# Sparse experts: in three of eight groups the expert with the fewest tokens changes places with the last one, and the last one is put into the conditional second round

## The chip, the cores and the metric

The kernel runs on one core of a Trainium2 chip. The metric is device time in microseconds for one execution; lower is better. Several runs of a kernel are given by their median.

## The reference

The reference is two transformer blocks on 256 tokens of width 1024, all in fp32. The first block is dense. The second has a mixer and then a mixture of experts, which is what the change is about:

```python
MOE_GROUPS, EXPERTS_PER_GROUP, TOP_K, D_FF_EXPERT = 8, 8, 2, 512
group_logits = t @ w_router_group                      # 256 x 8
g_sel   = argmax(group_logits)                         # one group for a token
in_group = (t @ w_router_expert).reshape(n, 8, 8)[rows, g_sel]
top_logit, top_local = lax.top_k(in_group, 2)          # two experts of that group
gate = softmax(top_logit) * softmax(group_logits)[g_sel]
...
hid = silu(xb @ w_gate[e]) * (xb @ w_up[e])            # 1024 -> 512
y  += gate * (hid @ w_down[e])                         # 512 -> 1024
```

There are 64 experts. The three matrices of one have 3 x 1024 x 512 fp32 values, 6.29 MB. The 256 tokens give 512 pairs of token and expert, so an expert has 8 tokens on average, and some may have none.

## The kernel before

Everything up to the mixture of experts is the same in both kernels. The experts run in `moe` (L1339), from about 657 us to about 1630 us of the profile.

Groups are processed as **visits**. `plan` (L1120) counts the tokens of each group and sorts them: group 0 is always at place 0, the others follow by size at places 1 to 7. `which` (an int32 copy of `at_`) holds the group at each place. The first visit is group 0 with experts 0 to 2, whose names are known without any counting; then come places 1, 2, 3, 7, 4, 5, 6 with eight experts each, and last group 0 again with experts 3 to 7. That makes 64 expert steps, numbered i = 0 to 63. `in_order` (L1499) gives the index of an expert for a load, from a register that SP reads from `which`.

A group at places 0 to 6 is "small": 64 token slots. Each small group's tokens are gathered by a matmul with a one-hot matrix (`prepare`, L1221; `slot2`, `keys`), split into a high and a low fp32r part and held as the 128 stationary columns `xghi` (64 slots, high and low). Place 7 has 128 slots and three passes in place of two. After the last expert of a visit `summed` (L1317) scatters the result into `xres`.

One expert step is 12 chunks: four of `w_gate`, four of `w_up`, four of `w_down` of the expert before. A chunk (128 x 1024) is split by ACT (`whi`) and DVE (`wlo`) in `split` (L104, L107), except that the fourth chunk of `w_down` is used as it is (L1389). The chunks are fetched three ahead (`AHEAD`). There are six buffers of `whi` and `wlo`. From chunk s = 8 on, the order of PE, ACT and DVE is the order of the program text; before it a scheduler orders them, and what stands under `soon()` has priority.

The weights are loaded by SP in six DMAs of 1 MB for an expert, into a ring of 11 slots (L1492 to L1496). SP issues in program order, and a load waits until its slot has been read. A load carries a condition from the third expert on (`wanted`, L1267): SP reads the number of the expert's tokens from `manyx` into a register, and where it is 0 the DMA is issued but moves nothing. The rest of the expert's step is carried out all the same, on whatever the slot holds, with gate weights of zero.

`weights` (L1093) computes the gate weights `wsel` (token x expert in its group), `count` (L1194) the tokens of each expert, `beyond` (L1156) whether a group has more tokens than slots, in small DVE instructions that are mixed into the steps from s = 121 on. `flag` is 1 when some group has. Then a **second round** (L1516 to L1518) runs two more groups, 16 experts with 128 slots; else it is jumped over.

Of the kernel before, what the change touches and what calls it, by code (L numbers as in the profile page):

```python
# [9 lines left out]
F32 = mybir.dt.float32  # L10
# [22 lines left out]
def mega(ctx, tc, a, out, dbg=None):  # L33
# [1059 lines left out]
    def weights():  # L1093
# [23 lines left out]
        nc.vector.tensor_tensor(wsel, o1, o2, op=OP.add)  # L1117
        dump("wsel", wsel)

    def plan():  # L1120
        ps = mm.tile([P, 512], F32, tag="mm", name="pct")
        for t in range(NT):
            nc.tensor.matmul(ps[:, :8], ones, G[:, t, :], start=t == 0, stop=t == 1)

        c64 = lambda n: mp.tile([P, 8, 8], F32, name=n)
        col = lambda x: x[:, :, None].to_broadcast([P, 8, 8])
        lin = lambda x: x[:, None, :].to_broadcast([P, 8, 8])
        size = mp.tile([P, 8], F32, name="size")
        nc.vector.scalar_tensor_tensor(size, ps[:, :8], 16.0, rdx, op0=OP.mult, op1=OP.add)
        nc.vector.memset(size[:, 0:1], -1.0)  # L1130
        gidx = mp.tile([P, 8], F32, name="gidx")
        nc.vector.tensor_scalar(gidx, rdx, -1.0, 8.0, op0=OP.mult, op1=OP.add)
        perm = c64("perm")
        nc.vector.tensor_tensor(perm, lin(size), col(size), op=OP.is_lt)
        place = mp.tile([P, 8], F32, name="place")
        nc.vector.tensor_reduce(place, perm, AX.X, OP.add)

        nc.vector.tensor_scalar(base, place, NG - 1.0, float(P - GS), op0=OP.is_equal, op1=OP.mult)
        nc.vector.tensor_scalar(base, base, float(GS), None, op0=OP.add)
        nc.vector.tensor_tensor(over, ps[:, :8], base, op=OP.subtract)  # L1140
        nc.vector.tensor_tensor(perm, col(gidx), lin(place), op=OP.is_equal)
        work = c64("work")
        nc.vector.tensor_tensor(work, perm, lin(gidx), op=OP.mult)
        at_ = mp.tile([P, 8], F32, name="at_")
        nc.vector.tensor_reduce(at_, work, AX.X, OP.add)
        nc.vector.tensor_copy(which, at_)
        for t in range(NT):
            nc.vector.tensor_tensor(work, perm, lin(G[:, t, :]), op=OP.mult)
            nc.vector.tensor_reduce(keys[:, t, :], work, AX.X, OP.add)
        nc.vector.tensor_copy(keys_, keys)  # L1150
        nc.vector.tensor_scalar(keys, keys, -4096.0, 4096.0, op0=OP.mult, op1=OP.add)
        nc.vector.tensor_tensor(keys, keys, b8(rank), op=OP.add)
# [3 lines left out]
    def beyond():  # L1156

        b1 = lambda n, w=1: mp.tile([P, w], F32, name=n)
        r, at, ovi, off, mem = b1("bey_r", 8), b1("bey_at", 8), b1("ovi", 3), b1("bey_off"), r8("bey_mem")
        nc.vector.tensor_scalar(r, over, 0.0, None, op0=OP.is_gt)  # L1160
        nc.vector.tensor_tensor(r, r, rdx, op=OP.mult)
        for x in range(2):
            m, key = ovi[:, 1 + x:2 + x], keyx[x]
            nc.vector.tensor_reduce(m, r, AX.X, OP.max)
            if x:
                nc.vector.tensor_scalar(off, over[:, 0:1], float(P), None, op0=OP.is_gt)
                nc.vector.tensor_scalar(at[:, 0:1], off, 8.0, None, op0=OP.mult)
                nc.vector.tensor_tensor(m, m, at[:, 0:1], op=OP.max)
                nc.vector.scalar_tensor_tensor(base[:, 0:1], off, float(P), base[:, 0:1], op0=OP.mult, op1=OP.add)
            else:  # L1170
                nc.vector.tensor_scalar(ovi[:, 0:1], m, 0.0, None, op0=OP.is_gt)
            yield
            nc.vector.tensor_tensor(at, rdx, m.to_broadcast([P, 8]), op=OP.is_equal)
            for t in range(NT):
                nc.vector.tensor_tensor(mem[:, t, :], G[:, t, :], at, op=OP.mult)
            nc.vector.tensor_reduce(key, mem, AX.X, OP.add)
            nc.vector.tensor_scalar(key, key, -4096.0, 4096.0, op0=OP.mult, op1=OP.add)
            nc.vector.tensor_tensor(key, key, rank, op=OP.add)
            yield
            nc.vector.tensor_tensor(mem[:, 0, :], at, base, op=OP.mult)  # L1180
            nc.vector.tensor_reduce(off, mem[:, 0, :], AX.X, OP.add)
            nc.vector.tensor_tensor(key, key, off.to_broadcast([P, NT]), op=OP.subtract)
            if x == 0:
                nc.vector.tensor_tensor(at, at, r, op=OP.mult)
                nc.vector.tensor_tensor(r, r, at, op=OP.subtract)
            yield
        nc.vector.tensor_scalar(ovi[:, 1:3], ovi[:, 1:3], -1.0, 8.0, op0=OP.mult, op1=OP.add)
        nc.vector.tensor_scalar(ovi[:, 1:3], ovi[:, 1:3], NG - 1.0, None, op0=OP.min)
        nc.vector.tensor_copy(ovx, ovi)
        for _ in range(6):  # L1190
            yield
        beyonds["flag"] = nc.values_load(ovx[0:1, 0:1], min_val=0, max_val=1, skip_runtime_bounds_check_because="it is 0 or 1")

    def count():  # L1194

        for t in range(NT):
            nc.vector.tensor_tensor(sel[:, t], keys_[:, t, :, None].to_broadcast([P, 8, 8]),
                                    osel[:, t, None, :].to_broadcast([P, 8, 8]), op=OP.mult)
        ps = mm.tile([P, 512], F32, tag="mm", name="pct")
        for t in range(NT):  # L1200
            nc.tensor.matmul(ps[:, :64], ones, sel[:, t].rearrange("p g e -> p (g e)"), start=t == 0, stop=t == 1)
        nc.vector.tensor_copy(manyx, ps[:, :64])

    ev = lambda w: w.rearrange("e (p k) n -> p e k n", p=P)
    wg, wu, wd = ev(a["w_gate_2"]), ev(a["w_up_2"]), ev(a["w_down_2"])
# [12 lines left out]
    def two(x):  # L1218
        return x.rearrange("p k (a b) -> p k a b", a=2)

    def prepare(keys, b, small, xgs, gws, v):  # L1221

        oh = mq.tile([P, NT, P], F32, name="oh", bufs=1)
        for t in range(NT):
# [111 lines left out]

    AHEAD = 3

    def moe(keys, expert, visits, small=lambda g: False, skip=False, begin=(), on_the_way=iter(())):  # L1339

        todo = [(v, g, e, es) for v, (g, es) in enumerate(visits) for e in es]
        n = len(todo)
        plain = lambda i: skip and small(todo[i][1]) and i < n - 2
# [70 lines left out]
        def follow(s):  # L1417

            i, kind, c = order[s]
            v, g, e, es = todo[i]  # L1420
            last = s + 1 == len(order) or order[s + 1][:2] != (i, kind)
            if kind in "gu":
                if last:
                    steps.append([1, copied(i, kind)])
                if kind == "u" and last and e == es[max(0, len(es) - 4)] and v + 1 < len(visits):
                    g2 = visits[v + 1][0]
                    steps.append([1, prepare(keys(g2), (v + 1) % 2, small(g2), xgs, gws, v + 1)])
                if i == 0 and kind == "u" and last:
                    finish(steps)
                    steps.append([1, turned(hids, 0, gus.pop(0), gws[v][0], small(g), plain(0))])  # L1430
                return
            if i + 1 < n and (last if i + 2 < n else c == 1):
                g1 = todo[i + 1][1]
                hl = None
                if i + 2 == n:
                    finish(steps)
                    hl = [x[:, (todo[i + 1][0] + 1) % 2, :4] for x in xgb]
                x = turned(hids, i + 1, gus.pop(i + 1), None, small(g1), plain(i + 1), hl)
                if i + 2 == n:
                    finish([[0, x]])  # L1440
                else:
                    steps.append([next(x), x])
            if last and e == es[-1] and i < n - 1:
                steps.append([1, summed(pds.pop(v), gws[v][1])])
# [5 lines left out]
            gens.clear()  # L1450

        with soon():
            prep = prepare(keys(visits[0][0]), 0, small(visits[0][0]), xgs, gws, 0)
            while 0 not in xgs:
                next(prep)
            for f in begin[:2]:
# [40 lines left out]
    bases = {}  # L1497

    def in_order(g, e):  # L1499
        if g == 0:  # L1500
            return e
        if g not in bases:
            bases[g] = value(which[0:1, g:g + 1], NG - 1)
        return bass.ds(bases[g] * NE + e, 1)
# [1 line left out]

    every = list(range(NE))
    moe(lambda g: [(keys[:, t, g:g + 1] if g else key0[:, t:t + 1]) for t in range(NT)], in_order,
        [(0, every[:3])] + [(g, every[3 * (g == 0):]) for g in (1, 2, 3, 7, 4, 5, 6, 0)],
        small=lambda g: g < NG - 1, skip=True, begin=(plan, weights, count), on_the_way=beyond())  # L1510


    flag = beyonds["flag"]
    again = [nc.values_load(ovx[0:1, x:x + 1], engines=(mybir.EngineType.SP,), min_val=0, max_val=NG - 1,
                            skip_runtime_bounds_check_because="a group's index") for x in (1, 2)]
    with tc.If(flag > 0):  # L1516
        moe(lambda x: [keyx[x][:, t:t + 1] for t in range(NT)], lambda x, e: bass.ds(again[x] * NE + e, 1),
            [(0, every), (1, every)])  # L1518
    dump("h2", xres)
    g_nf = row(a["norm_final_2"], D, "g_nf")  # L1520
    ms = [mean_sq(ssf[:, t, :]) for t in range(NT)]
# [54 lines left out]
```

## Time and profile before

| | |
|---|---|
| three runs | 1646.37 us median (1645.75 to 1648.77) |
| the profiled execution | 1646.35 us, of which the trace spans 1644.6 us |
| mean granted TensorE clock | 0.989 of full speed |
| PE, DVE, ACT busy | 98%, 82%, 70% of the span |

PE is TensorE's matmuls, PEld its weight loads, DVE is VectorE, ACT ScalarE, POOL GpSimd, SP SyncE. Busy time of PE is modelled from pipelined matmuls. The trace says for each instruction when it began, how long it took, and what ended the idle time before it.

### The profile page before, as it was taken

To read this page: it belongs to the slowest core of one execution; us is meant where nothing else is said; L and a number is where in the kernel's file an instruction comes from. 1 tells how busy PE (TensorE), PEld (TensorE's weight loads), DVE (VectorE), ACT (ScalarE), POOL (GpSimd) and SP (SyncE) were. 2 spreads that over 40 slices of the span, in tenths; PEclk is the share of its full clock that TensorE was granted. 3 is DMA by queue.
4 is the path that set the end of the run, shared out by engine and by line. 5 is a ranking of instruction groups with operands and counts; after the bars stand their busy time and mean duration, and the time that the engine had idled before them with its cause. 6 is when DMAs were issued, how large, how long until landed. Compare 5 with 4: busy or idle time off the path is not lost. (4 is left out here: it accounts for less than half of the span.)

```text
span 1644.6 us, 24374 instructions
## 1 busy us (share of the span) xinstructions
PE 1606.0 (98%) x8474; PEld 1302.4 (79%) x8474; DVE 1353.3 (82%) x1643; ACT 1148.5 (70%) x1544; POOL 44.7 (3%) x69
## 2 busy tenths in 40 slices
PE   8999999999999998999999999999999999999996
PEld 7898788998798877777767777778877777777774
DVE  6666675555868886799999999998999899999997
ACT  5355554444556643788878888877788888888886
POOL 1000010000100130000000000000000000000000
PEclk9999999999999998999999999999999999999999
DMA  9953455555663337797997999999999999999991
GB/s 323 273 175 130 142 171 201 180 189 170 173 182 122 116 132 298 271 421 325 385 392 315 380 421 421 421 412 363 347 380 420 409 421 420 421 420 420 421 375 48
DMA packets 124884, 493.55 MB, mean 300 GB/s; under 512 B 9149, under 2 KB 53537, under 8 KB 78160
## 3 DMA queue, kind: packets, MB, share of 16 engines
q1 hardware_dynamic: 120160, 484.47, 76.9%
q0 software_dynamic: 1952, 6.05, 1.3%
q10 hardware_dynamic: 2640, 1.38, 0.3%
q8 instruction: 69, 1.13, 0.3%
q14 instruction: 63, 0.52, 0.1%
HBM read 509.30 MB, written 1.44 MB: 311 GB/s over the span
## 5 line engine op out<-in xcount | busy, mean ns | idle before, releaser
L107 DVE TENSOR_TENSOR wlo<-ring,whi 128x1024 fp32r<-128x1024 f32 x714 | 839.9, 1219 | 63.4 <-ACT whi L107 59.8
L107 ACT CAST whi<-ring 128x1024 fp32r<-128x1024 f32 x714 | 712.3, 1048 | 74.0 <-PE pgu L1279 20.9
L1279 PE MATMUL pgu<-whi,xghi 128*128 128x512 f32 x896 | 356.6, 398 | 1.4 <-DVE xghi L1216 1.4
L1280 PE MATMUL pgu<-wlo,xghi 128*128 128x512 f32 x896 | 352.8, 394 | 1.1 <-DVE wlo L107 1.1
L107 DVE TENSOR_TENSOR wlo<-raw,whi 128x1024 fp32r<-128x1024 f32 x173 | 211.8, 1232 | 135.6 <-ACT whi L107 134.3
L107 ACT CAST whi<-raw 128x1024 fp32r<-128x1024 f32 x173 | 180.3, 1048 | 188.9 <-PE pb L115 81.0
L1280 PEld LDWEIGHTS pgu<-wlo,xghi 128*128 128x128 f32 x896 | 169.4, 189 | 37.4 <-DVE wlo L107 3.4
L1279 PEld LDWEIGHTS pgu<-whi,xghi 128*128 128x128 f32 x896 | 169.4, 189 | 35.3 <-DVE xghi L1216 1.6
L114 PE MATMUL pb<-hThi,whi 128*128 128x256 f32 x480 | 137.5, 286 | 0.2 <-ACT hThi L129 0.2
L1279 PE MATMUL pd<-whi,hidThi 128*128 128x512 f32 x332 | 136.5, 411 | 0.9 <-DVE hidThi L1299 0.8
L115 PE MATMUL pb<-hTlo,whi 128*128 128x256 f32 x480 | 135.8, 283 | 0.5 <-DVE hTlo L130 0.5
L116 PE MATMUL pb<-hThi,wlo 128*128 128x256 f32 x480 | 135.7, 283 | 0.0
L1280 PE MATMUL pd<-wlo,hidThi 128*128 128x512 f32 x332 | 130.9, 394 | 0.0
L1289 PEld LDWEIGHTS pht<-pairs,gu 128*128 128x128 f32 x896 | 108.6, 191 | 4.9
L1289 PE MATMUL pht<-pairs,gu 128*128 128x64 f32 x896 | 106.0, 271 | 0.0
L1389 PE MATMUL pd<-ring,hs 128*64 128x512 f32 x216 | 104.2, 605 | 0.0
L1279 PEld LDWEIGHTS pd<-whi,hidThi 128*128 128x128 f32 x332 | 62.2, 187 | 52.8 <-ACT whi L107 36.1
L115 PEld LDWEIGHTS pb<-hTlo,whi 128*128 128x128 f32 x480 | 91.9, 191 | 1.4 <-DVE hTlo L130 0.7
L114 PEld LDWEIGHTS pb<-hThi,whi 128*128 128x128 f32 x480 | 91.9, 191 | 1.2 <-ACT hThi L129 0.5
L116 PEld LDWEIGHTS pb<-hThi,wlo 128*128 128x128 f32 x480 | 91.8, 191 | 0.0
L114 PE MATMUL pa<-whi,hThi 128*128 128x512 f32 x216 | 87.0, 406 | 3.3 <-ACT whi L107 1.7
L116 PE MATMUL pa<-whi,hTlo 128*128 128x512 f32 x216 | 85.6, 399 | 1.2 <-DVE hTlo L130 1.2
(432 smaller groups left out, 2260.1 us busy)
## 6 DMA issues: line engine op xcount, KB each, us to landing
ring<-in_w_gate_dram SPq DMA_DIRECT2D x128, 1024.0 KB, 9.9
ring<-in_w_up_dram SPq DMA_DIRECT2D x128, 1024.0 KB, 10.6
ring<-in_w_down_dram SPq DMA_DIRECT2D x126, 1024.0 KB, 9.2
raw<-in_w_in_dram SPq DMA_DIRECT2D x38, 1024.0 KB, 5.4
raw<-in_w_ff_dram SPq DMA_DIRECT2D x32, 1024.0 KB, 5.0
raw<-in_w_out_dram SPq DMA_DIRECT2D x12, 1024.0 KB, 5.0
raw<-in_w_in_dram SPq DMA_DIRECT2D x9, 512.0 KB, 4.8
raw<-in_w_ple_gate_dram SPq DMA_DIRECT2D x4, 1024.0 KB, 5.0
```

The costliest lines, as they stand in the source:

```text
L107: both = [nc.scalar.copy(hi, raw), nc.vector.tensor_tensor(lo, raw, hi.bitcast(F32), op=OP.subtract)]
L114: nc.tensor.matmul(ps, l[0][lsel], r[0][rsel], start=first, stop=False)
L115: nc.tensor.matmul(ps, l[0][lsel], r[1][rsel], start=False, stop=False)
L116: nc.tensor.matmul(ps, l[1][lsel], r[0][rsel], start=False, stop=last)
L1279: nc.tensor.matmul(ps, x[0][:, k, :], w[0][wsel], start=first, stop=False)
L1280: nc.tensor.matmul(ps, x[0][:, k, :], w[1][wsel], start=False, stop=last)
L1289: nc.tensor.matmul(ps[:, j, q, :], x[:, ts(q)], pairs, start=True, stop=True)
L1389: nc.tensor.matmul(pds[v][m][:GS, :], h[:, 3, :], wt[:, 0, cols(m)], start=False, stop=False)
```

## The change

`count` still counts the tokens of each expert, but in a float tile `many`. For the places 0, 1 and 2 (`NS = 3`) it finds the expert with the fewest tokens, the one with the higher index first where several have as few (in group 0 experts 0 to 2 are left out, since their loads have begun by then). `trade` exchanges that expert's column with column 7, in the counts, in the names of the experts and, for the tokens of these groups, in the gate weights. The names go to `namesx`, the exchanged gate weights to `wsel2`, and the largest of the three counts that now stand in column 7 to `left`.

The first round then runs 7 experts in place of 8 in the visits of places 1 and 2, and 4 in place of 5 in the last visit of group 0: 61 steps in place of 64. The expert of column 7 of these three groups moves behind the condition of the second round, as three `moe` calls of one expert each. `flag` is 1 when a group has too many tokens or `left` is above 0.

```diff
@@ plan: at_ is made outside, the 64-wide tiles get a tag each
+    at_ = mp.tile([P, 8], F32, name="at_")
@@ beyond
-                nc.vector.tensor_scalar(ovi[:, 0:1], m, 0.0, None, op0=OP.is_gt)
+                nc.vector.tensor_tensor(ovi[:, 0:1], m, left, op=OP.max)
+                nc.vector.tensor_scalar(ovi[:, 0:1], ovi[:, 0:1], 0.0, None, op0=OP.is_gt)
@@
+    def trade(x, at, n):
+        d, both = mp.tile([P, n, 8], F32, name="trd"), mp.tile([P, n], F32, name="trs")
+        nc.vector.tensor_tensor(d, x[:, :, 7:8].to_broadcast([P, n, 8]), x, op=OP.subtract)
+        nc.vector.tensor_tensor(d, d, at, op=OP.mult)
+        nc.vector.tensor_reduce(both, d, AX.X, OP.add)
+        nc.vector.tensor_tensor(x, x, d, op=OP.add)
+        nc.vector.tensor_tensor(x[:, :, 7], x[:, :, 7], both, op=OP.subtract)
@@ count
-        nc.vector.tensor_copy(manyx, ps[:, :64])
+        many = mp.tile([P, 8, 8], F32, tag="work", name="many")
+        nc.vector.tensor_copy(many, ps[:, :64].rearrange("p (g e) -> p g e", g=8))
+        few2 = mp.tile([P, 2, NS, 8], F32, tag="perm", name="few")
+        few, few3 = few2[:, 0], few2[:, 1]
+        by3 = lambda x: x[:, None, :].to_broadcast([P, NS, 8])
+        nc.vector.scalar_tensor_tensor(few, many[:, :NS], 16.0, by3(rdx), op0=OP.mult, op1=OP.add)
+        nc.vector.memset(few[:, 0, :3], 1e6)
+        fewest = mp.tile([P, NS], F32, name="fewest")
+        nc.vector.tensor_reduce(fewest, few, AX.X, OP.min)
+        nc.vector.tensor_tensor(few, few, fewest[:, :, None].to_broadcast([P, NS, 8]), op=OP.is_equal)
+        names = mp.tile([P, NS, 8], F32, name="names")
+        nc.vector.tensor_scalar(names, by3(rdx), -1.0, 8.0, op0=OP.mult, op1=OP.add)
+        trade(many[:, :NS], few, NS)
+        trade(names, few, NS)
+        nc.vector.scalar_tensor_tensor(names, at_[:, :NS, None].to_broadcast([P, NS, 8]), 8.0, names, op0=OP.mult, op1=OP.add)
+        nc.vector.tensor_copy(manyx, many.rearrange("p g e -> p (g e)"))
+        nc.vector.tensor_copy(namesx, names)
+        nc.vector.tensor_reduce(left, many[:, :NS, NE - 1], AX.X, OP.max)
+        mine = mp.tile([P, NT, 8], F32, tag="ing", name="mine")
+        for t in range(NT):
+            nc.vector.tensor_tensor(few3, few, keys_[:, t, :NS, None].to_broadcast([P, NS, 8]), op=OP.mult)
+            nc.vector.tensor_reduce(mine[:, t, :], few3.rearrange("p g e -> p e g"), AX.X, OP.add)
+        nc.vector.tensor_copy(wsel2, wsel)
+        trade(wsel2, mine, NT)
@@ prepare takes wsel as an argument: the first visit's is wsel, the later ones' wsel2
@@ in_order
-        if g == 0:
-            return e
+        if g < NS:
+            return bass.ds(value(namesx[0:1, g, e:e + 1], NG * NE - 1), 1) if g or e > 2 else e
@@ the visits
-        [(0, every[:3])] + [(g, every[3 * (g == 0):]) for g in (1, 2, 3, 7, 4, 5, 6, 0)],
+        [(0, every[:3])] + [(g, every[3 * (g == 0):NE - (g < NS)]) for g in (1, 2, 3, 7, 4, 5, 6, 0)],
@@ behind the first round
+    lasts = [nc.values_load(namesx[0:1, x, NE - 1:NE], engines=(mybir.EngineType.SP,), min_val=0, max_val=NG * NE - 1,
+                            skip_runtime_bounds_check_because="an expert's index") for x in range(NS)]
     with tc.If(flag > 0):
+        for x in range(NS):
+            moe(lambda g: [(keys[:, t, g:g + 1] if g else key0[:, t:t + 1]) for t in range(NT)],
+                lambda g, e: bass.ds(lasts[g], 1), [(x, [NE - 1])], small=lambda g: True)
         moe(lambda x: [keyx[x][:, t:t + 1] for t in range(NT)], lambda x, e: bass.ds(again[x] * NE + e, 1),
-            [(0, every), (1, every)])
+            [(0, every), (1, every)], wsel=wsel)
```

## Rows read from the trace of the kernel before

**Rows 1.** The page's busy time by engine, share of the span, count.
```profile
PE 1606.0 (98%) x8474; PEld 1302.4 (79%) x8474; DVE 1353.3 (82%) x1643; ACT 1148.5 (70%) x1544; POOL 44.7 (3%) x69
```

**Rows 2.** Windows: length, busy PE, PEld, DVE, ACT, POOL, clock, DMA share, GB/s.
```profile
1537.32:1551.25 13.93, 13.93 (x65) 10.43 (x65) 13.26 (x14) 12.32 (x16) 0.00 (x0) 1.00 1.01 418
775.07:896.69 121.62, 119.56 (x559) 88.58 (x559) 114.79 (x147) 100.38 (x124) 0.00 (x0) 1.00 0.91 363
896.69:1014.31 117.62, 117.62 (x559) 89.33 (x559) 111.00 (x116) 101.17 (x125) 0.00 (x0) 1.00 0.99 401
1273.68:1391.22 117.54, 117.54 (x559) 89.32 (x559) 110.71 (x115) 100.59 (x124) 0.00 (x0) 1.00 1.01 416
1391.22:1508.79 117.57, 117.57 (x559) 89.32 (x559) 110.71 (x115) 100.58 (x124) 0.00 (x0) 1.00 1.01 421
```

**Rows 3.** Timeline of SP's queue late in the visit of place 6: start, length, what.
```profile
1537.32 1.16 SPq L99 DMA_DIRECT2D ring<-in_w_down_dram  x2
...
1551.25 1.05 SPq L99 DMA_DIRECT2D ring<-in_w_down_dram  x2
```

**Rows 4.** Tile ring, gate loads in 598:759, 759:763, 881:885, 1566:1571; ns min/median/max.
```profile
L99 SPq DMA_DIRECT2D ring<-in_w_gate_dram x18: 327/333/508, 598.6 to 748.3; - x18
...
L99 SPq DMA_DIRECT2D ring<-in_w_gate_dram x2: 79/86/92, 759.6 to 761.9; - x2
...
L99 SPq DMA_DIRECT2D ring<-in_w_gate_dram x2: 84/84/84, 881.8 to 883.7; - x2
...
L99 SPq DMA_DIRECT2D ring<-in_w_gate_dram x2: 84/84/84, 1567.2 to 1569.5; - x2
```

**Rows 5.** Tile ring, landing times, windows 740:760, 1180:1200, 1240:1260, 1480:1500, 1560:1566.
```profile
DMA to landing us min/median/max: 10.8/11.0/11.1
...
DMA to landing us min/median/max: 4.9/5.0/5.1
...
DMA to landing us min/median/max: 9.2/9.4/9.6
...
DMA to landing us min/median/max: 15.9/16.1/16.3
...
DMA to landing us min/median/max: 16.5/17.4/18.4
```

**Rows 6.** Tile ring over the whole span: casts and the loads of w_down.
```profile
L107 ACT CAST whi<-ring x714: 1032/1048/1071, 620.7 to 1625.8; 128x1024 fp32r<-128x1024 f32 x179
...
L99 SPq DMA_DIRECT2D ring<-in_w_down_dram x130: 84/333/1020, 612.2 to 1603.9; - x130
```

**Rows 7.** Timeline around `count`: start, length, what.
```profile
659.35 0.22 DVE L1202 CAST manyx<-pct 128x64 int32<-128x64 f32 x1 [0.39 <-PE pct L1201]
...
661.39 1.23 DVE L107 TENSOR_TENSOR wlo<-ring,whi 128x1024 fp32r<-128x1024 f32 x1 [1.81 <-ACT whi L107]
...
667.13 0.47 PE L1280 MATMUL pgu<-wlo,xghi 128*128 128x512 f32 x1
...
668.50 0.47 PE L1280 MATMUL pgu<-wlo,xghi 128*128 128x512 f32 x1
```

**Rows 8.** Timeline of DVE: two stretches of small instructions, in `plan` and `beyond`.
```profile
653.71 0.22 DVE L1148 TENSOR_TENSOR work<-perm,G 128x64 f32<-128x64 f32 x1
...
654.73 0.17 DVE L1150 COPY keys__6020<-keys 128x16 f32<-128x16 f32 x1
...
814.43 0.16 DVE L1173 TENSOR_TENSOR bey_at<-rdx,ovi 128x8 f32<-128x8 f32 x1
...
816.16 1.23 DVE L107 TENSOR_TENSOR wlo<-ring,whi 128x1024 fp32r<-128x1024 f32 x1
```

**Rows 9.** SP: its register loads, and its queue in the visit of place 7.
```profile
L1259 SPq TENSOR_LOAD <-manyx x61: 263/269/293, 668.3 to 1581.6; - x61
...
1105.33 3.07 SPq L99 DMA_DIRECT2D ring<-in_w_down_dram  x2
...
1122.29 0.33 SPq L99 DMA_DIRECT2D ring<-in_w_down_dram  x1
```

More of the change, by code (lines that the diff above doesn't have):

```diff
@@ L1123, in plan @@
             nc.tensor.matmul(ps[:, :8], ones, G[:, t, :], start=t == 0, stop=t == 1)
-        c64 = lambda n: mp.tile([P, 8, 8], F32, name=n)
+        c64 = lambda n: mp.tile([P, 8, 8], F32, tag=n, name=n)
         col = lambda x: x[:, :, None].to_broadcast([P, 8, 8])
@@ L1143, in plan @@
         nc.vector.tensor_tensor(work, perm, lin(gidx), op=OP.mult)
-        at_ = mp.tile([P, 8], F32, name="at_")
         nc.vector.tensor_reduce(at_, work, AX.X, OP.add)
@@ L1192, in beyond @@
         beyonds["flag"] = nc.values_load(ovx[0:1, 0:1], min_val=0, max_val=1, skip_runtime_bounds_check_because="it is 0 or 1")
+    NS = 3
+    namesx = mp.tile([P, NS, 8], I32, name="namesx")
+    left = mp.tile([P, 1], F32, name="left")
+    wsel2 = r8("wsel2")
+    def trade(x, at, n):
[5 more added lines that the diff above has]
+        nc.vector.tensor_tensor(x[:, :, 7], x[:, :, 7], both, op=OP.subtract)
     def count():
@@ L1219, in two, with prepare @@
         return x.rearrange("p k (a b) -> p k a b", a=2)
-    def prepare(keys, b, small, xgs, gws, v):
+    def prepare(keys, b, small, xgs, gws, v, wsel):
         oh = mq.tile([P, NT, P], F32, name="oh", bufs=1)
@@ L1337, in mega, with moe @@
     AHEAD = 3
-    def moe(keys, expert, visits, small=lambda g: False, skip=False, begin=(), on_the_way=iter(())):
+    weights_ = wsel
+    def moe(keys, expert, visits, small=lambda g: False, skip=False, begin=(), on_the_way=iter(()), wsel=wsel2):
+        first = weights_ if skip else wsel
         todo = [(v, g, e, es) for v, (g, es) in enumerate(visits) for e in es]
@@ L1426, in follow @@
                     g2 = visits[v + 1][0]
-                    steps.append([1, prepare(keys(g2), (v + 1) % 2, small(g2), xgs, gws, v + 1)])
+                    steps.append([1, prepare(keys(g2), (v + 1) % 2, small(g2), xgs, gws, v + 1, wsel)])
                 if i == 0 and kind == "u" and last:
@@ L1452, in moe @@
         with soon():
-            prep = prepare(keys(visits[0][0]), 0, small(visits[0][0]), xgs, gws, 0)
+            prep = prepare(keys(visits[0][0]), 0, small(visits[0][0]), xgs, gws, 0, first)
             while 0 not in xgs:
```

## The prediction

> **What bounds the kernel now.** The first view is the busy time by engine: PE 98%, DVE 82% [rows 1]. That is an average over a long dense part too, so the second view is the windows of the expert stage alone. One expert step in the middle of a visit takes 13.93 us, for which PE is busy without a gap (65 matmuls), DVE for 13.26 us, ACT for 12.32 us, and the DMA engines all of it, at 418 GB/s [rows 2]. Three resources are full or nearly so, and this view does not say which of them sets the pace.
>
> The third view, the loads, does. An expert is 6.29 MB; at 421 GB/s that is 6.29 / 0.421 = 14.94 us of DMA, yet steps follow each other every 13.93 us, read off the same load of successive experts in SP's queue [rows 3]. So compute runs ahead of the DMA inside a visit, and the DMA catches up at the visits' ends: eight experts take 117.54 or 117.57 us, that is 8 x 13.93 = 111.4 and 6.1 more for gathering and scattering, 14.69 us for an expert [rows 2]. The DMA still loses 0.25 us an expert. The time from issue to landing shows it: 9.2 to 9.6 us early in the visit of place 4, 15.9 to 16.1 two visits later, 17.4 at its worst [rows 5]. Does anyone wait for it? A slot comes round after 11 loads, 11/6 x 13.93 = 25.5 us; it is held while it is read, two casts of 1.05 and the subtract behind them, some 3.5 us. A load has therefore about 22 us (an estimate from these rows). The last loads agree: issued up to 1603.9, the last chunk cast at 1625.8, 21.9 us later [rows 6]. 17.4 is below 22: compute sets the pace, and PE within it.
>
> Who is empty? A load whose condition fails takes 79 to 92 ns to issue instead of 333. The first such pair of gate loads follows 18 full ones, so it is expert step 9; the second is at 881.8, 122 us or eight steps on, step 17; the third at 1567.2, step 62 [rows 4]. These are the seventh experts of places 1 and 2 and of group 0. The reference's router on its own inputs says the same: groups of 12, 22, 40, 36, 46, 17, 6 and 77 tokens, and the only three experts of all 64 with none are number 6 of groups 0, 6 (place 1) and 5 (place 2). An empty expert gets no bytes but all its compute: the stretch 896.69 to 1014.31, in which step 17 is computed, has the same 559 matmuls and takes 117.62 us, as against 117.54 where all eight have tokens [rows 2].
>
> **The change, part by part.** *Removed:* three expert steps. In each of the three groups the fewest is 0 tokens, it changes places with expert 7, and `left` is 0. What goes is 3 x 13.93 = 41.79 us of compute [rows 2, 3] and 18 loads that moved nothing. The gathering and scattering at the visits' ends stay, as the number of visits does. `todo` still ends in two steps with fully split `w_down`, so the tail is built as before.
>
> *What the DMA does then.* The same 61 experts are loaded, in less time. Until now an empty expert gave the DMA a pause: landing was at 11.0 us at 740 to 760, before step 9 [rows 5]. Without pauses a visit of seven takes 7 x 13.93 + 6.1 = 103.6 us and needs 7 x 14.94 = 104.6 of DMA, so landing grows by 1.0 in each of the first two and by 2.0 in the one of place 3: from 11 to about 15. In the visit of place 7 a step takes 1122.29 - 1105.33 = 16.96 us [rows 9], and the DMA empties its queue; landing is back at 5 by 1180 [rows 5]. From there nothing changes until step 62, whose pause is gone. There the queue is 18.4 us behind, and six more loads at 2.49 against 2.32 us add 1: 19.4, under 22. Counted as bytes: loads issued at 1565.9 go out 27.9 us earlier, at 1538, and land by 1556.4; the 8 MB that follow need 8 x 2.49 = 19.9, so all has landed by 1576.3, and the last cast is due at 1625.8 - 41.8 = 1584.0. I cost it at 0; the cover is 2.6 to 7.7 us.
>
> The Trainium skill, page "DMA: Bandwidth & Descriptors", section "Where 436 GB/s comes from", speaks against the change: for loads from HBM it lets the HBM side bind at about 358 GB/s. By that an expert would need 17.6 us, DMA would be the bound, and dropping experts without bytes would give nothing. The trace disagrees, with 421 GB/s held over whole visits [rows 2]; what the rule would do here is the second rival below.
>
> *Added in `count`:* 30 DVE instructions for 1, nearly all in a chain. Not in the trace; by the nearest rows, four 64-wide ones take (654.73 - 653.71)/4 = 0.255 us each, eleven of 8 elements (816.16 - 814.43)/11 = 0.157 [rows 8]. These have 24 to 64, so 30 take 4.7 to 7.7 us; I take 6.0. They begin when the counts come, at 659.35, and end at 665.4; the subtract that began at 661.39 is held back by 4.0 us [rows 7]. It makes the seventh chunk (the first six fill the buffers), which PE multiplies at 667.13, and it would now end at 666.6; the eighth, needed at 668.50, at 667.8. So it is nearly hidden: 0, and 1.1 at the long end. Without that cover all of it counts: at the price of `beyond`, where 32 more DVE instructions (147 against 115) cost 121.62 - 117.57 = 4.05 us, 0.127 each [rows 2], 29 would be 3.7. I take 0.6. SP's reads of `manyx` and `namesx` come long after, since the loads of step 3 wait for slots.
>
> *Moved: `beyond`.* It is tied to s = 121, the middle of step 10. That was the last step of place 1; now it is the first of place 2, and the scatter of the ended visit follows at once. DVE has 0.67 us to spare in a step, and a visit's end gives it 110.71 - 8 x 13.26 = 4.6 us of work more, as against 6.1 for PE [rows 2]. At best the two overlap (6.1 - 4.6 = 1.5 gained), at worst all 4.6 falls on the path. In an undisturbed visit PE's 6.1 covers DVE's 4.6, so I stay near that end: 1.0, and 0.1 for the one instruction more.
>
> *Added on SP:* 18 register reads from `namesx` and 3 of `lasts`, less 2 of `which`, at 0.27 us [rows 9], 5.1 us over 950, in a queue that waits for slots. Behind such a read stands one gate load, late by at most 0.27 us, a tenth of the narrowest margin above: 0. *In the second round:* code that is jumped over, by the same one branch: 0.
>
> **The sum** is made against the profiled execution, 1646.35 us, 0.02 below the median of the three runs: 1646.35 - 41.79 + 0.6 + 1.1 = 1606.3.
>
> **The rivals.**
> *The second round runs* (slower). It decides as soon as one of the three traded experts has a single token. Then `flag` is 1, and not only three experts run but all of the second round: 16 steps at 16.96 and three visits of one expert at 13.93 + 6.1, 271 + 60 = 331 us, about 1937. Against it stand the three skipped loads, one in each of the three groups [rows 4].
> *The loads set the pace, and nothing is gained.* All 61 experts with tokens are loaded as before; were DMA the bound, the time stayed at 1646. For it: DMA is full in nearly every window at 421 GB/s. Against it: the stretches with and without an empty expert take the same time, and landing stays under 22 us.
> *The loads become the bound at the end.* If the lead is 17 and not 22, the last experts wait up to 19.4 - 17 = 2.4 us, and the visit of place 3 not at all: about 1609.
> *The small DVE work is all exposed:* 3.7 for `count` and 4.6 for `beyond` on a visit's end in place of 1.6: 1646.35 - 41.79 + 8.4 = 1613.0; half of it is likelier than the whole, about 1609.5.
> *`beyond` falls in better than before:* 1.5 gained, `count` hidden: 1603.1.
>
> **How the numbers follow.** The sum as worked out, 1604 to 1608: 0.70. DVE exposed, 1608 to 1613: 0.12. Loads binding at the end: 0.06. Better placed, 1602.8 to 1604: 0.06. Loads set the pace: 0.03. Second round: 0.03. The forecast is 1606.3. The range takes in the best case and DVE's exposure up to 1612: 1602.8 to 1612.0. A measurement of this kernel tells about 0.2% (3 us) from no change. All cases but the loads' and the second round's are faster: 0.94; same 0.03; slower 0.03.
>
> **What would show it.** 61 expert steps, 53 of them small (53 x 16 = 848 matmuls of L1279 into `pgu`), no ring load under 300 ns, the step still 13.93 us, landing 15 to 20 us late in the stage, and the last seven-expert visit about 103.6 us long. Wrong would be: landing at 22 and casts waiting for the ring; PE idle near 667 or after 812; work of the second round behind the last expert.

## The result and the profile after

The changed kernel takes 1605.16 us (median of 4 runs, 1603.59 to 1606.52), the kernel before, run beside it, 1646.97 (1645.75 to 1648.77). The ratio is 0.9745, 95% interval 0.9728 to 0.9762: 2.5% faster, 41.8 us. The forecast was 1606.3.

The profiled execution took 1605.47 us with a span of 1603.7. The page's busy time answers to [rows 1], and its queue and its largest group of matmuls show the 61 steps:

```profile
PE 1564.9 (98%) x8282; PEld 1271.0 (79%) x8282; DVE 1316.5 (82%) x1634; ACT 1111.3 (69%) x1499; POOL 44.6 (3%) x69
...
q1 hardware_dynamic: 120160, 484.47, 78.3%
...
L1321 PE MATMUL pgu<-whi,xghi 128*128 128x512 f32 x848 | 338.1, 399 | 1.4 <-DVE xghi L1258 1.4
```

848 matmuls are 53 small experts of 16, three fewer than 56. The load queue moved 484.47 MB, as it did in the kernel before, so no expert with tokens was dropped:

```profile
q1 hardware_dynamic: 120160, 484.47, 76.9%
```

The engines' shares are what they were, to within a point; an average over the span says nothing of this change, since three steps of the average kind were taken out.

The windows answer to [rows 2]: one step, then three stretches that begin and end at the same place of a visit: the pause in SP's loads while PE gathers the tokens of the next visit, in the fourth expert from a visit's end. Each stretch holds one gathering and one scattering.

```profile
1524.62:1538.56 13.94, 13.94 (x65) 10.43 (x65) 13.27 (x14) 12.32 (x16) 0.00 (x0) 1.00 1.01 420
761.40:869.84 108.44, 105.65 (x495) 78.11 (x495) 101.78 (x135) 88.14 (x109) 0.00 (x0) 1.00 1.00 410
869.84:987.52 117.68, 117.68 (x559) 89.28 (x559) 111.03 (x116) 101.19 (x125) 0.00 (x0) 1.00 1.01 416
1247.00:1364.51 117.51, 117.51 (x559) 89.17 (x558) 110.61 (x115) 100.57 (x124) 0.00 (x0) 1.00 1.01 417
```

A step is still 13.94 us. The first stretch has seven steps where [rows 2] has eight in 121.62: less 13.93 that would be 107.69, and it takes 0.75 more. PE stands idle for 2.79 us of it, as against 2.06 in [rows 2]. What PE waited for there, in the changed kernel and then in the kernel before (waited for, us in total, times, longest):

```profile
PE pd L1321 <- DVE hidThi L1341: 1.2, 2, 0.7
PE pgu L1322 <- DVE wlo L107: 1.0, 3, 0.4
PE psct L1371 <- DVE yglo L130: 0.5, 1, 0.5
...
PE pgu L1280 <- DVE wlo L107: 1.1, 3, 0.4
PE pd L1279 <- DVE hidThi L1299: 0.8, 1, 0.8
```

The third wait is new: it is the scatter's matmul (`psct`), which waits for DVE. The other two stretches have eight steps and the length that they had. The loads, over the whole span (answering to [rows 4] and [rows 6]), and their landing times in 740:760, 960:980 and 1540:1560 (answering to [rows 5]):

```profile
L107 ACT CAST whi<-ring x681: 1027/1047/1069, 620.8 to 1585.3; 128x1024 fp32r<-128x1024 f32 x171
...
L99 SPq DMA_DIRECT2D ring<-in_w_gate_dram x122: 327/333/795, 598.7 to 1542.9; - x122
...
DMA to landing us min/median/max: 9.0/11.1/11.8
...
DMA to landing us min/median/max: 11.1/12.9/14.3
...
DMA to landing us min/median/max: 15.5/17.9/19.2
```

No load is short any more: the quickest gate load takes 327 ns to issue, so none failed its condition. Landing, the time from a load's issue until its data are there, climbs to 14.3 us before the visit of place 7 and to 19.2 at the end, where 15 and 19.4 were forecast. Only the first filling of the ring, near 620 us, has longer ones, up to 22.5; it has them in the kernel before as well (22.8). The last cast, at 1585.3, comes 40.5 us earlier than in [rows 6].

The new work of `count`, in DVE's timeline (the rows answer to [rows 7]), and the two PE matmuls that could have waited for it:

```profile
659.45 0.22 DVE L1222 COPY many<-pct 128x64 f32<-128x64 f32 x1 [0.39 <-PE pct L1218]
...
661.54 0.17 DVE L1242 TENSOR_REDUCE mine<-few 128x8 f32<-128x24 f32 x1
661.63 1.21 DVE L107 TENSOR_TENSOR wlo<-ring,whi 128x1024 fp32r<-128x1024 f32 x1
662.76 0.17 DVE L1207 TENSOR_REDUCE trs<-trd 128x3 f32<-128x24 f32 x1
...
668.80 0.15 DVE L1209 TENSOR_TENSOR wsel<-wsel,trs 128x2 f32<-128x2 f32 x1
```

```profile
667.55 0.48 PE L1322 MATMUL pgu<-wlo,xghi 128*128 128x512 f32 x1
...
668.69 0.48 PE L1322 MATMUL pgu<-wlo,xghi 128*128 128x512 f32 x1
```

The chain did not run as one block ahead of the subtracts. Eighteen instructions fill the gap in which DVE used to wait, and the subtract of the seventh chunk begins 0.24 us later than before, not 4.0; the rest stands in small groups between the next subtracts. The eighth chunk is multiplied at 668.69, 0.19 later than before. Of that 0.10 was there already when the counts came (659.45 against 659.35), and the other 0.09 arose near 664.2, ahead of both matmuls: PE was busy without a gap in both kernels, but the granted clock rose from 0.50 to 1.00 of full speed (1.2 to 2.4 GHz) a little later than before. The same stretch in the changed kernel and in the kernel before:

```profile
664.00:664.40 0.40, 0.40 (x2) 0.33 (x1) 0.40 (x2) 0.40 (x1) 0.00 (x0) 0.50 0.00 0
...
664.00:664.40 0.40, 0.40 (x3) 0.36 (x2) 0.32 (x1) 0.40 (x1) 0.00 (x0) 0.89 0.00 0
```

### The profile page after: what moved, and what is told of

The parts are those of the page before. It is cut to its first block, busy times and chain, and to the rows that moved or that the text cites. A ratio compares the mean times of both kernels' runs of the same rounds, so it can differ in the third digit from the quotient of the medians.

```text
span 1603.7 us, 23716 instructions
## 1 busy us (share of the span) xinstructions
PE 1564.9 (98%) x8282; PEld 1271.0 (79%) x8282; DVE 1316.5 (82%) x1634; ACT 1111.3 (69%) x1499; POOL 44.6 (3%) x69
## 3 DMA queue, kind: packets, MB, share of 16 engines
q1 hardware_dynamic: 120160, 484.47, 78.3%
## 5 line engine op out<-in xcount | busy, mean ns | idle before, releaser
L107 DVE TENSOR_TENSOR wlo<-ring,whi 128x1024 fp32r<-128x1024 f32 x681 | 801.8, 1220 | 59.7 <-ACT whi L107 55.9
L107 ACT CAST whi<-ring 128x1024 fp32r<-128x1024 f32 x681 | 679.8, 1047 | 72.5 <-PE pgu L1321 19.6
L1321 PE MATMUL pgu<-whi,xghi 128*128 128x512 f32 x848 | 338.1, 399 | 1.4 <-DVE xghi L1258 1.4
L1322 PE MATMUL pgu<-wlo,xghi 128*128 128x512 f32 x848 | 333.6, 393 | 1.0 <-DVE wlo L107 1.0
L1322 PEld LDWEIGHTS pgu<-wlo,xghi 128*128 128x128 f32 x848 | 160.4, 189 | 35.0 <-DVE wlo L107 2.7
L1321 PEld LDWEIGHTS pgu<-whi,xghi 128*128 128x128 f32 x848 | 160.4, 189 | 33.8 <-DVE xghi L1258 1.6
L1321 PE MATMUL pd<-whi,hidThi 128*128 128x512 f32 x314 | 128.8, 410 | 1.2 <-DVE hidThi L1341 1.2
L1322 PE MATMUL pd<-wlo,hidThi 128*128 128x512 f32 x314 | 123.9, 395 | 0.0
L1331 PEld LDWEIGHTS pht<-pairs,gu 128*128 128x128 f32 x848 | 102.8, 191 | 4.6
L1434 PE MATMUL pd<-ring,hs 128*64 128x512 f32 x204 | 98.4, 605 | 0.0
```

Source lines behind the costliest of these rows:

```text
L107: both = [nc.scalar.copy(hi, raw), nc.vector.tensor_tensor(lo, raw, hi.bitcast(F32), op=OP.subtract)]
L1321: nc.tensor.matmul(ps, x[0][:, k, :], w[0][wsel], start=first, stop=False)
L1322: nc.tensor.matmul(ps, x[0][:, k, :], w[1][wsel], start=False, stop=last)
L1331: nc.tensor.matmul(ps[:, j, q, :], x[:, ts(q)], pairs, start=True, stop=True)
L1434: nc.tensor.matmul(pds[v][m][:GS, :], h[:, 3, :], wt[:, 0, cols(m)], start=False, stop=False)
```

## The experiments

Each ratio is to runs of the kernel before on the same chip. Where a time is set against the changed kernel's 1605.16 us, the two were not run side by side.

**Counting and exchanging, but no step taken out** (from the changed kernel):

```diff
-        [(0, every[:3])] + [(g, every[3 * (g == 0):NE - (g < NS)]) for g in (1, 2, 3, 7, 4, 5, 6, 0)],
+        [(0, every[:3])] + [(g, every[3 * (g == 0):]) for g in (1, 2, 3, 7, 4, 5, 6, 0)],
```

> The changed kernel with all eight experts left in the first round: the counting, the exchange of columns and the wider flag are there, the three steps are not taken out. The empty expert of each of the three groups is now the last of its visit. Theory (a step costs its compute, and the 29 new DVE instructions are hidden): 64 steps again, 0 to 1 us over the kernel before, about 1647.5. Rival (small DVE work is exposed as that of beyond is): 3.7 us more, about 1650.7.

1646.59 us against 1646.19, ratio 1.0005 (0.9996 to 1.0014). The upper end is 2.3 us: 3.7 us of exposed instructions are excluded, a cost up to 2.3 is not told from nothing. The stretch with the instructions of `beyond` and the one after it:

```profile
773.16:894.98 121.82, 119.79 (x559) 88.55 (x559) 114.95 (x148) 100.37 (x124) 0.00 (x0) 1.00 0.92 366
894.98:1012.66 117.68, 117.68 (x559) 89.28 (x559) 111.03 (x116) 101.21 (x125) 0.00 (x0) 1.00 0.93 375
```

The first takes 0.20 us more than in [rows 2], for one small instruction more (148 against 147). So the whole gain lies in the steps taken out.

**The empty experts loaded after all** (from the kernel before):

```diff
     def wanted(i):
-        if i is None:
-            return {}
+        return {}
```

> The kernel before with no condition on any load: the three empty experts get their 6.29 MB each, 18.9 MB more in all. Theory (compute sets the pace and the loads have 22 us): no longer than before, 1646 to 1649, with landing times that no longer fall around 780, 900 and 1580 and reach about 19 us at the end. Rival (the loads set the pace): 3 x 14.94 = 44.8 us more, about 1692.

1645.48 us against 1646.19, ratio 0.9996 (0.9986 to 1.0005): 18.9 MB more, and no time. The landing times in 740:760, 980:1000 and 1580:1600, and the gate loads:

```profile
DMA to landing us min/median/max: 8.3/10.6/12.2
...
DMA to landing us min/median/max: 11.6/14.2/15.6
...
DMA to landing us min/median/max: 16.2/18.2/19.2
...
L99 SPq DMA_DIRECT2D ring<-in_w_gate_dram x128: 327/333/582, 598.5 to 1585.4; - x128
```

All 128 gate loads are full, and landing near 1580 stays at 16 to 19 us, which is still in time. An empty expert therefore cost its compute alone.

**One group instead of three** (from the changed kernel):

```diff
-    NS = 3
+    NS = 1
```

> The change for group 0 alone (NS = 1): one step less, the last but one. Theory: 13.93 us less and 0.2 for the counting, about 1633.2, and, since place 1 keeps its eight experts, no 0.75 us more in the visit in which the instructions of beyond run. Rival (the gain is not per step but comes from the early visits, where the loads paused): less than 3 us.

1632.3 us (1630.74 to 1634.96), 13.9 less than before, ratio 0.9919 (0.9903 to 0.9934): one step, one time 13.93. The visit of place 1 keeps its eight experts, and the stretch in which `beyond` runs does not get the 0.75 us:

```profile
773.21:894.97 121.76, 119.67 (x559) 88.66 (x559) 114.97 (x148) 100.40 (x124) 0.00 (x0) 1.00 0.91 363
```

**The instructions of `beyond` one by one** (from the changed kernel; in `beyond` a `yield` stands behind every DVE instruction, and none elsewhere):

```diff
-                if s > 120:
+                if s > 120 and s % 3 == 0:
                     next(on_the_way, None)
```

> The changed kernel with the 33 DVE instructions of beyond handed out one at a time, one to every third chunk from s = 121 on, in place of three to eleven at once. Theory (they cost 4.05 us, and 0.75 more in the changed kernel, because they come in a burst that leaves DVE no spare time; a step has 0.67 us of it, three chunks 0.17, and an instruction takes 0.16): nearly all of it comes back, 4.8 us less, about 1600.4; at least 3. Rival (DVE work costs its time wherever it stands): no change, 1605.2.

1600.27 us (1599.57 to 1603.86), ratio to the kernel before 0.9725 (0.9711 to 0.9738), 4.9 us less than the median of the changed kernel. That stretch of seven steps, which took 108.44 us, now is

```profile
760.28:864.36 104.08, 104.05 (x495) 78.72 (x495) 98.37 (x116) 88.17 (x109) 0.00 (x0) 1.00 1.01 418
```

4.36 us shorter, close to the 103.6 of seven undisturbed steps with one gathering and one scattering, and PE is idle for 0.03 us of it. Only 14 of the 33 small instructions still fall into it; the other 19 fall into the next stretch, which is no longer for them than the 117.68 us that it took without:

```profile
864.36:982.03 117.67, 117.67 (x559) 89.26 (x559) 112.27 (x135) 101.17 (x125) 0.00 (x0) 1.00 1.01 420
```

The 33 small instructions cost nearly nothing once no more than one of them stands between two subtracts. As the two medians were not taken side by side, both kernels were run once more on one chip, unchanged:

> The changed kernel once more, beside the one with beyond spread out, on one chip: 1605 us, ratio 0.975.

> The version with the instructions of beyond handed out one by one, on the same chip as the changed kernel. Theory (a burst costs, single instructions do not): 4.4 us (the shortening of its visit by the traces) under the changed kernel, 1600 to 1601. Rival (the difference seen between two chips is their scatter): within 2 us of it.

The changed kernel took 1607.81 us (1605.54 to 1608.03, ratio 0.9761, 0.9747 to 0.9776), the one with `beyond` spread out 1600.98 (1599.25 to 1603.89, ratio 0.9724, 0.9708 to 0.9741). The intervals are apart: this version is faster than both kernels. The medians differ by 6.8 us where the traces gave 4.4; as runs of one kernel lie up to 4.6 us apart here, the size is not told closer than that.

**Fewer slots** (from the changed kernel: 9 without the two `atT` buffers, and 7 without two more):

```diff
-    for x in ("hi", "lo"):
-        ring.append(tt.tile([P, 4 * F], F32, tag="atT" + x, name="ring"))
```

> The changed kernel with 9 ring slots in place of 11. Theory (a load has the time of one turn of the ring less 3.5 us; landing reaches 19.2 us late in the stage, 14.3 before the visit of place 7): 9/6 x 13.93 - 3.5 = 17.4 us, passed once, by 1.8 us: about 1607, and casts that wait for the ring near the end. Rival (the lead is far longer than the landing times): no change, 1605.2.

> The changed kernel with 7 ring slots in place of 11. Theory: 7/6 x 13.93 - 3.5 = 12.8 us, passed in the visit of place 3 by 1.5 us and at the end by 6.4: about 8 us more, 1613, with waits for the ring in those two places. Rival (the lead is far longer than the landing times): less than 2 us more.

Nine slots: 1605.89 us (1605.54 to 1608.16), 0.7 more than the changed kernel's median and inside its spread, ratio 0.9751; two casts wait for the ring, at 1552 and 1557, 1.2 us in all. (The changed kernel's list has such waits between 1080 and 1180 only, of at most 0.4 us, where landing is short.) Seven slots: 1612.03 us (1611.47 to 1612.91), 6.9 more, ratio 0.9785 (0.977 to 0.98). The waits of ACT for the ring, first with nine, then with seven:

```profile
ACT whi L107 <- DMA ring<-in_w_gate_dram: 0.7, 1, 0.7
ACT whi L107 <- DMA ring<-in_w_up_dram: 0.5, 1, 0.5
```

```profile
ACT whi L107 <- DMA ring<-in_w_gate_dram: 10.3, 10, 1.4
ACT whi L107 <- DMA ring<-in_w_up_dram: 7.6, 18, 1.7
```

Landing over the whole span, with nine and with seven:

```profile
DMA to landing us min/median/max: 4.8/11.3/18.8
...
DMA to landing us min/median/max: 4.8/10.9/15.1
```

With seven, landing never passes 15.1 us, as a load waits for its slot before it is issued. At nine and at seven slots the times are what the ring's turn less 3.5 us forecast, to about 1 us, and the changed kernel has some two slots to spare.

**Less work for PE**, to see what is next:

```diff
-                        nc.tensor.matmul(pds[v][m][:GS, :], h[:, 3, :], wt[:, 0, cols(m)], start=False, stop=False)
+                        m or nc.tensor.matmul(pds[v][m][:GS, :], h[:, 3, :], wt[:, 0, cols(m)], start=False, stop=False)
```

> The changed kernel without half of the matmuls of the fourth w_down chunk (L1434, the second half of the columns): two of four in each of 51 steps, 0.97 us of PE, so columns 512 to 1023 of the output lack that chunk's part. Every load, cast and subtract stays. Theory (PE sets the pace now, and the loads are next, 2.8 us behind it at the end and 7.7 before the visit of place 7): of 51 x 0.67 = 34 us that DVE's 13.26 us a step would allow, only some 10 come, about 1594, with casts that wait for the ring. Rival (the loads are no bound): 34 us less, about 1571.

1586.83 us (1585.3 to 1589.83): 18.3 less, between the two forecasts, ratio 0.963 (0.9616 to 0.9645). A step of the visit of place 4 and one of the visit of place 6, and the longest waits of casts for the ring, all of them behind 1440:

```profile
1261.95:1275.03 13.08, 13.08 (x63) 10.17 (x63) 12.84 (x14) 11.89 (x16) 0.00 (x0) 1.00 1.01 420
...
1493.03:1507.92 14.89, 14.37 (x69) 10.96 (x69) 13.53 (x14) 12.41 (x16) 0.00 (x0) 1.00 1.01 420
```

```profile
ACT whi L107 <- DMA ring<-in_w_gate_dram: 5.0, 5, 1.4
...
ACT whi L107 <- DMA ring<-in_w_up_dram: 3.0, 7, 0.9
```

The step falls by 0.85 us at first, more than the 0.67 that was expected (DVE's busy time falls with it, so 13.26 was no floor). Late in the stage a step takes 14.89 us, which is 6.29 MB at 422 GB/s; PE is idle for 0.5 us of it, and casts wait for the ring: there the loads set the pace. The Trainium skill, page "DMA: Bandwidth & Descriptors", section "Where 436 GB/s comes from", lets loads from HBM bind at about 358 GB/s; this run, in which they do bind, gives 420 over that step, near the 425 that the same section names for a measurement of 16 MB.

**The second round, always run** (from the changed kernel):

```diff
-                nc.vector.tensor_scalar(ovi[:, 0:1], ovi[:, 0:1], 0.0, None, op0=OP.is_gt)
+                nc.vector.tensor_scalar(ovi[:, 0:1], ovi[:, 0:1], 0.0, None, op0=OP.is_ge)
```

> The changed kernel with the flag always 1: the comparison with 0 is at least in place of greater than, so the second round runs, on experts without tokens, as it would run wholly for any input in which one of the three traded experts had a token. It measures the price of the rival that was on the other side: 331 us by the prediction's rows (16 x 16.96 and 3 x 20.0), about 1936. With less overlap from step to step or loads that are not prefetched across its four moe calls it would be 20 to 60 us more.

1983.66 us in the one run, 378.5 more than the changed kernel, 47 beyond the sum of steps. SP's queue shows where: the gate loads of the three single experts, and the first, the fourth and two late ones of the 16 that follow.

```profile
1567.94 0.96 SPq L99 DMA_DIRECT2D ring<-in_w_gate_dram  x2
...
1585.31 1.47 SPq L99 DMA_DIRECT2D ring<-in_w_gate_dram  x2
...
1608.91 1.77 SPq L99 DMA_DIRECT2D ring<-in_w_gate_dram  x2
...
1637.67 1.47 SPq L99 DMA_DIRECT2D ring<-in_w_gate_dram  x2
...
1703.38 3.26 SPq L99 DMA_DIRECT2D ring<-in_w_gate_dram  x2
...
1808.31 3.12 SPq L99 DMA_DIRECT2D ring<-in_w_gate_dram  x2
...
1825.25 3.13 SPq L99 DMA_DIRECT2D ring<-in_w_gate_dram  x2
```

From one single expert to the next it is 17.4 and 23.6 us, from the third to the first of the 16 it is 28.8, and the first three of the 16 take 65.7, where 50.9 were counted; late ones keep to 16.94, near the 16.96 of the visit of place 7 [rows 9]. Each `moe` call fills and empties its own chain of chunks, and in these gaps not only PE stands idle:

```profile
1600.00:1640.00 40.00, 33.12 (x154) 26.79 (x152) 29.29 (x36) 26.60 (x38) 0.00 (x0) 0.89 0.62 221
1640.00:1680.00 40.00, 30.79 (x124) 25.41 (x125) 23.06 (x28) 20.45 (x33) 0.00 (x0) 0.75 0.66 252
```

PE is idle for 6.9 and 9.2 us of 40, the DMA moves little more than half of what it can, and the granted clock, the number before the last two, falls from 1.00 to 0.89 and 0.75 of full speed on average. How much of the 47 us each accounts for was not settled. So the gain of 41.8 us hangs on the data. By this one run, with one token in one of the three exchanged experts the kernel would take about 337 us longer than the kernel before.

## Why the prediction was right

*Compute sets the pace, and a step without tokens costs 13.93 us.* Right, and shown from three sides: three steps fewer give 41.8 us, one fewer gives 13.9, and 18.9 MB more of loads give nothing. The windows alone had not decided this, as PE, DVE and DMA all looked full; the landing times against the turn of the ring did.

*The loads stay in time.* Right. Landing reached 19.2 us for a forecast of 19.4. The rule behind the lead of 22 us holds to about 1 us with nine and with seven slots; the 22 itself stays an estimate, since with eleven no cast waited late in the stage. (The prediction's 17.4 "at its worst" is a median in [rows 5]; the longest there is 18.4, the figure that its forecast of 19.4 starts from.) The rival in which loads bind at the end did not come; with seven slots it does, and with PE relieved it does.

*`count` is hidden: 0.6.* Right that it is hidden, and the way there was pessimistic. It was taken as one block of 6 us ahead of the subtracts, nearly used up by the slack; the scheduler put 18 instructions into a gap and scattered the rest. By the timeline PE is 0.09 us later behind it, and that came with the clock at 664 and not with a wait for the chain; by the timing of the run with 64 steps it is under 2.3 us.

*`beyond` beside the scatter: 1.1.* It measured 0.75 in its stretch (108.44 against 107.69), about 0.2 of it for the instruction more, as the runs with eight experts in that visit show (0.14 and 0.20). The rest goes where the visit of place 1 keeps its length, and nearly all of it goes, with the 4.05 us of before, where the instructions are spread. PE's waits show where it lies: the scatter now follows at once, and its matmul waits 0.5 us for DVE, a wait that neither the kernel before nor the two runs with eight experts in that visit have. One sign of the prediction left the 4.05 us out: the stretch of seven steps took 108.44 us and not 103.6, as it has the instructions of `beyond` in it; spread out it takes 104.08.

*The sum.* The spans differ by 40.9 us, so 0.9 of the 41.79 was given back, where 1.7 was forecast: both small terms were set too high.

*The second round* was priced at 331 us and costs 378. The late steps were right; the filling and emptying of three more `moe` calls and of the last was left out, and with it the clock that falls in these gaps.

In the run with less work for PE the room that the loads leave was mis-sized: 18.3 us came where 10 were expected. The traces' spans differ by 15.7 us. Of these 10.4 were won ahead of the visit of place 7 (the scatter at its start begins at 1045.34 us and not at 1055.77), where 7.7 were counted, none in that visit, and 5.3 behind it, where 2.8 were. The step shrank by 0.85 and not 0.67, and landing rose to 20.7 us before the visit of place 7. Why more came than the counted room of the loads was not settled.

## What to carry to other kernels

When several resources look full, compare the time from issue to landing with the time that a buffer takes to come round: it tells who waits for whom, and how far the loads are from binding. Work on data that turns out empty costs its full compute even where its loads are skipped, so it pays to skip the compute as well. Small instructions on a nearly full engine cost their time when they come in a burst and almost nothing when they are handed out one at a time, and a shortcut that hangs on the data needs the price of its other branch beside its gain.

## What was not expected of the hardware

In the kernel before, a load whose condition fails still takes 73 to 92 ns of SP's queue, as against 333 for one that moves 1 MB. With less work for PE the loads held 418 to 423 GB/s, step after step, from 1400 to 1538, where they were the bound; with 7 slots it was 420 in the windows 1440:1480 and 1500:1540, where casts waited as well. Thirty-two small DVE instructions of 0.14 to 0.17 us each cost 4.05 us of the stage in a burst, though DVE was busy for 13.26 of 13.93 us in a step and had, over a visit of 117.57 us, 6.6 to spare. And where PE stood idle between the short `moe` calls of the second round, the granted clock fell to 0.75 on average over 40 us.
